# State-space parameters and rotation table on the Pool engine, eight state-space units started later, and small column work moved between engines, in a hybrid recurrent decoder step

## The chip, the cores and the metric

One core of a Trainium2 chip runs the whole program in one launch. The metric is device microseconds from start to end of an execution, lower is better. PE is the matrix engine, DVE the vector engine, ACT the scalar (activation) engine, POOL the general engine that the code calls `G` (`nc.gpsimd`), SP the engine that issues the DMAs. In the code `PE`, `V`, `S` and `G` stand for PE, DVE, ACT and POOL.

## What is computed

One step of a decoder layer on 544 tokens (one prompt of 512, and 8 samples of 4), 1,024 channels, float32, cut to what matters here:

```python
z = x @ w_in                                   # then split into 9 parts
# A: gated linear recurrence on 512 channels
xa_c = causal_conv4(xa);  gx, ga = sigmoid(gate matmuls of xa_c)
a  = exp(-8 * ga * softplus(-lambda))
bx = sqrt(1 - a*a) * (gx * xa_c)
h[t] = a[t]*h[t-1] + bx[t];   out_a = (h * gelu(ya)) @ proj_a
# B: short gated convolution
out_b = (sb * causal_conv3(sc * sh)) @ proj_b
# C: diagonal complex state space, 32 groups of 16 channels, 64 states each
step = exp(log_dt);  abar = exp(step * (a_re + i*a_im))
bbar = (abar - 1) / (a_re + i*a_im) * b
s[t] = abar * s[t-1] + bbar @ u[t];   y = Re(c @ s) + d * u
out_c = glu(gelu(y)) @ proj_c
x = LN(alpha*x + sigmoid-gated merge of out_a, out_b, out_c @ w_out)
x = LN(alpha*x + mlp(x))
```

The last states of A, B and C are outputs too.

## The kernel before

Every float32 matmul is done in three passes over a high and a low half of each operand. For the weights, the high half is an ACT cast (`wh`, L114 and later L819) and the low half a DVE subtraction (`wl`, L115 and L820). Weights are split two blocks ahead.

The program first computes `us`, the input of C, and then 20 blocks of `z`, one after the other, numbered by `ti`: 0 to 7 alternate between `xa` (with the convolution, `a_conv`) and `ya` (`gy`, a gelu on ACT), 8 to 11 are `sb`, 12 to 19 alternate between `sc` and `sh`. 20 to 27 are merge blocks. The text calls them tiles. One tile is 48 matmuls (two halves of the tokens, eight blocks of channels, three passes) into one of four rotating PSUM buffers (`big`), and ACT or DVE takes the result out. After tile `ti`, `run_side(ti)` writes out the side work that the table `at(...)` has put there; this table, and the order of the code, set the order on each engine, for each engine runs its instructions in the order in which they stand. The side work is:

- the gates of branch A (`a_gate`, after tiles 2, 4, 6, 8): a pair of small matmuls, on ACT three tanh (`tx` L607, `ta` L611, `aT` L612), on DVE `bx` (L608); then `a_rec` (DVE: r = 1 - t, reciprocal, product), `a_sqrt` (ACT, `q`), `a_coef` (POOL 2r - 1 into `aT`, DVE product), `a_scan` (tile 13: DVE scans along the tokens, and ACT copies of the last columns into the state tile `st`, L639 and L642);
- the parameters of C (`params`, called ahead of the tiles, on DVE) and the rotation table `E_r`, `E_i` (`etable`, 128 powers per state by doubling: six operations for each of 7 steps m, steps 0 to 3 on DVE, 4 to 6 on POOL);
- eight units of C, each of two groups of states: `ssm_w` and `ssm_o` (POOL: coefficient matrices `wt` and `oo`), `ssm_a` (PE: four transposes and eight small matmuls; ACT copies `W`, and ten blocks into `M`; DVE adds the diagonal D to `M`, L479, twice), `ssm_b` (PE matmuls with `W`; DVE products with the table, scans, products; POOL adds `HP`), `ssm_c` (ACT copies of the last state column out of `HP`, L517 and L518; PE with `M`, `oo` and `HP`; ACT gelu). The lists `UA`, `UB`, `UC` name the tile after which a, b and c of each unit stand.

Large tiles (`gy`, `sbt`, `q`, `r`, `E_r`, `Et`, ...) come from a pool `slot` of 14 buffers, in turn: a new tile takes the buffer of the oldest one and waits for its last reader. All small values of `params` lie in one such tile, named `scr`; so do the sines and cosines that `etable` reads (`cn`, `sn`), up to its last step.

After the tiles come Strassen-like sums of the inputs `xq` (`t_sum`, four DVE subtractions of 128x1088) and of the weights `sr` (POOL), and the merges. The lines that matter most:

```python
UA = [10, 13, 15, 18, 20, 22, 23, 25]
UB = [a + 1 for a in UA]
UC = [a + (2 if a > 18 else 3) for a in UA]
...
            e = V if m < 4 else G
...
        S.copy(W.rearrange("p r j n -> p (r j n)"), wps)
...
        S.copy(st_lh[:, :, 0:NB], prev)
...
        S.copy(two(sbt[:, ct]), flat(ps))
```

Of the kernel before, what the change touches and what calls it, by code (L numbers as in the profile page):

```python
# [64 lines left out]
def kernel(ctx: ExitStack, tc: tile.TileContext, I, O):  # L65
# [185 lines left out]
    def precise_exp(dst, v, n, name):  # L251
# [3 lines left out]
        ts(V, r, v, -87.0, 88.0, ALU.max, ALU.min)
        ts(V, k, r, 1.4426950408889634, MAGIC, MUL, ADD)
        ts(V, k, k, MAGIC, None, SUB)
        V.scalar_tensor_tensor(r, k, -0.693359375, r, op0=MUL, op1=ADD)
        V.scalar_tensor_tensor(r, k, 2.12194440e-4, r, op0=MUL, op1=ADD)
# [1 line left out]
        ts(V, dst, r, cs[7], cs[6], MUL, ADD)
        for c in cs[5::-1]:
            tt(V, dst, dst, r, MUL)
            ts(V, dst, dst, c, None, ADD)
        ts(V, ii, k, 127.0, 8388608.0, ADD, MUL)
        tt(V, dst, dst, ii.bitcast(F32), MUL)
# [3 lines left out]
    def params():  # L270
# [52 lines left out]
        tt(V, r2, angf, angf, MUL)  # L323
        f = [1.0 / math.factorial(i) for i in range(13)]
        ts(V, snf, r2, f[9], -f[7], MUL, ADD)
        for c in (f[5], -f[3], 1.0):
            tt(V, snf, snf, r2, MUL)
            ts(V, snf, snf, c, None, ADD)
        tt(V, snf, snf, angf, MUL)
        ts(V, cnf, r2, -f[10], f[8], MUL, ADD)  # L330
        for c in (-f[6], f[4], -f[2], 1.0):
            tt(V, cnf, cnf, r2, MUL)
            ts(V, cnf, cnf, c, None, ADD)
        t4 = stemp(128)
        ts(V, t4, kk, 0.25, MAGIC, MUL, ADD)
        ts(V, t4, t4, MAGIC, None, SUB)
        V.scalar_tensor_tensor(kk, t4, -4.0, kk, op0=MUL, op1=ADD)
        V.scalar_tensor_tensor(t4, kk, -1.0, kk, op0=MUL, op1=ALU.max)
# [1 line left out]
        ts(V, ck, t4, -1.0, 1.0, MUL, ADD)  # L340
        ts(V, t4, t4, -1.0, 2.0, MUL, ADD)
        tt(V, kk, kk, t4, MUL)
        ta, tb = stemp(128), stemp(128)
        tt(V, ta, snf, kk, MUL)
        tt(V, tb, cnf, kk, MUL)
        tt(V, cnf, cnf, ck, MUL)
        tt(V, cnf, cnf, ta, SUB)
        tt(V, snf, snf, ck, MUL)
        tt(V, snf, snf, tb, ADD)
# [7 lines left out]
        def cmul(orr, oi, ar, ai, br, bi):  # L357
            tt(V, u1, ar, br, MUL)
            tt(V, u2, ai, bi, MUL)
            tt(V, orr, u1, u2, SUB)  # L360
            tt(V, u1, ar, bi, MUL)
            tt(V, u2, ai, br, MUL)
            tt(V, oi, u1, u2, ADD)

        tt(V, A_r[:, :, 0], mag, cn[:, 0], MUL)
        tt(V, A_i[:, :, 0], mag, sn[:, 0], MUL)
# [4 lines left out]
        tt(V, rho, mag, mag, MUL)  # L371
        tt(V, rho, rho, rho, MUL)
        dn, nr = stemp(16), stemp(16)
        tt(V, u1, C("are"), C("are"), MUL)
        tt(V, u2, C("aim"), C("aim"), MUL)
        tt(V, dn, u1, u2, ADD)
        V.reciprocal(dn, dn)
        ts(V, nr, A_r[:, :, 0], 1.0, None, SUB)
# [1 line left out]
        tt(V, u1, nr, C("are"), MUL)  # L380
        tt(V, u2, ni, C("aim"), MUL)
        tt(V, u1, u1, u2, ADD)
        tt(V, F_r[:, :, 3], u1, dn, MUL)
        tt(V, u1, ni, C("are"), MUL)
        tt(V, u2, nr, C("aim"), MUL)
        tt(V, u1, u1, u2, SUB)
        tt(V, F_i[:, :, 3], u1, dn, MUL)
# [1069 lines left out]
```

## Time and profile before

| | |
|---|---|
| median of 3 runs | 882.92 us (882.62 to 883.97) |
| the profiled execution | 881.24 us, its span 879.5 us |
| PE busy | 841.5 us, 96% of the span |
| DVE busy | 637.6 us (73%) |
| ACT busy | 370.4 us (42%) |
| POOL busy | 306.1 us (35%) |
| mean granted TensorE clock | 0.987 |
| chain that ended last, by engine | PE 65%, DVE 22%, issue 4%, ACT 4%, DMA 3%, POOL 2% |

Times of the profile are in the span's own microseconds. The rest of the profiled execution, 1.7 us, lies around the span. A granted clock of 1.00 is 2.4 GHz, 0.50 is 1.2 GHz; a mean between them is a stretch that had both.

### The profile page before, as it was taken

To read this page: it belongs to the slowest core of one execution; us is meant where nothing else is said; L and a number is where in the kernel's file an instruction comes from. 1 tells how busy PE (TensorE), PEld (TensorE's weight loads), DVE (VectorE), ACT (ScalarE), POOL (GpSimd) and SP (SyncE) were. 2 spreads that over 40 slices of the span, in tenths; PEclk is the share of its full clock that TensorE was granted. 3 is DMA by queue.
4 is the path that set the end of the run, shared out by engine and by line. 5 is a ranking of instruction groups with operands and counts; after the bars stand their busy time and mean duration, and the time that the engine had idled before them with its cause. 6 is when DMAs were issued, how large, how long until landed. Compare 5 with 4: busy or idle time off the path is not lost.

```text
span 879.5 us, 16024 instructions
## 1 busy us (share of the span) xinstructions
PE 841.5 (96%) x6516; PEld 831.1 (94%) x6516; DVE 637.6 (73%) x1036; ACT 370.4 (42%) x626; POOL 306.1 (35%) x289
## 2 busy tenths in 40 slices
PE   7998869989999899989999999999999999999996
PEld 7997769989999899989998999999999999999996
DVE  6879998876565866689857889666666666655656
ACT  4352515343333543454435775444344444444310
POOL 1044963764652354844000321322221313132122
PEclk9999989999999999999999999999999999999998
DMA  8341123122214353223645435333333333333302
GB/s 296 124 118 48 52 75 104 54 75 82 77 50 137 129 139 98 72 72 96 221 160 175 144 124 168 96 97 97 96 97 96 98 96 96 91 90 126 104 4 100
DMA packets 31594, 94.00 MB, mean 107 GB/s; under 512 B 3424, under 2 KB 9952, under 8 KB 31136
## 3 DMA queue, kind: packets, MB, share of 16 engines
q1 hardware_dynamic: 31232, 91.92, 33.1%
q8 instruction: 51, 0.84, 0.4%
q0 software_dynamic: 288, 1.05, 0.3%
q14 instruction: 23, 0.19, 0.1%
HBM read 88.24 MB, written 2.49 MB: 103 GB/s over the span
## 4 chain that ended last, share of the span: by engine, by line
PE 65%; DVE 22%; issue 4%; ACT 4%; DMA 3%; POOL 2%; SPq 0%; DVEq 0%; ACTq 0%; POOLq 0%
PE big L146 37%; PE big L854 22%; DVE wl L115 4%; ACT wh L114 1%; DVE scr L233 1%; PE big L1284 1%; PE big L1125 1%; DMA raw<-in_w_dram 1%; DVE bx L233 1%; DVE wl L820 1%; DVE cacc L591 1%; DVE r L625 1%; DMA xraw<-in_xT_dram 1%; POOL sr L233 1%; DVE rl L233 1%
## 5 line engine op out<-in xcount | busy, mean ns | idle before, releaser
L233 POOL TENSOR_TENSOR sr<-raw 128x512 f32<-128x512 f32 x38 | 61.1, 1630 | 243.2 <-DMA raw<-in_w_dram 172.4
L146 PE MATMUL big<-xh,wh 128*128 128x272 f32 (+2 forms) x544 | 117.0, 297 | 6.6 <-DVE wh L196 4.6
L854 PE MATMUL big<-Tt,wh 128*128 128x272 f32 x608 | 118.0, 291 | 3.8 <-DVE uu L233 1.9
L115 DVE TENSOR_TENSOR wl<-raw,wh 128x1024 fp32r<-128x1024 f32 x70 | 90.7, 1299 | 37.3 <-ACT wh L114 37.3
L146 PE MATMUL big<-xh,wl 128*128 128x272 f32 (+2 forms) x544 | 113.9, 291 | 2.9 <-DVE wl L820 2.9
L146 PE MATMUL big<-xl,wh 128*128 128x272 f32 (+2 forms) x544 | 114.1, 292 | 0.0
L820 DVE TENSOR_TENSOR wl<-raw,wh 128x1024 fp32r<-128x1024 f32 (+1 forms) x73 | 96.2, 1318 | 20.1 <-ACT wh L819 19.0
L819 ACT CAST wh<-raw 128x1024 fp32r<-128x1024 f32 (+1 forms) x73 | 68.4, 937 | 84.6 <-PE big L146 47.3
L854 PEld LDWEIGHTS big<-Tt,wh 128*128 128x128 f32 x608 | 96.8, 191 | 4.6 <-DVE uu L233 2.1
L146 PE MATMUL big<-fh,wh 128*128 128x272 f32 (+2 forms) x448 | 98.2, 289 | 0.6 <-ACT rl L1178 0.6
L146 PE MATMUL big<-fh,wl 128*128 128x272 f32 (+2 forms) x448 | 97.8, 288 | 0.0
L146 PE MATMUL big<-fl,wh 128*128 128x272 f32 (+2 forms) x448 | 97.7, 288 | 0.0
L114 ACT CAST wh<-raw 128x1024 fp32r<-128x1024 f32 x70 | 73.0, 1046 | 57.9 <-PE big L146 37.2
L146 PEld LDWEIGHTS big<-xh,wh 128*128 128x128 f32 x544 | 87.1, 193 | 7.6 <-ACT xh L195 4.5
L146 PEld LDWEIGHTS big<-xh,wl 128*128 128x128 f32 x544 | 86.0, 192 | 3.2 <-DVE wl L820 3.2
L854 PE MATMUL big<-Tt,wl 128*128 128x272 f32 x304 | 88.8, 292 | 0.0
L146 PEld LDWEIGHTS big<-xl,wh 128*128 128x128 f32 x544 | 86.5, 192 | 0.1
L146 PEld LDWEIGHTS big<-fh,wh 128*128 128x128 f32 x448 | 72.4, 188 | 0.9 <-ACT rl L1178 0.8
L820 DVE TENSOR_TENSOR wl<-sr,wh 128x1024 fp32r<-128x1024 f32 x38 | 48.1, 1267 | 34.5 <-ACT wh L819 34.5
L146 PEld LDWEIGHTS big<-fl,wh 128*128 128x128 f32 x448 | 72.4, 188 | 0.0
L146 PEld LDWEIGHTS big<-fh,wl 128*128 128x128 f32 x448 | 72.1, 189 | 0.0
L819 ACT CAST wh<-sr 128x1024 fp32r<-128x1024 f32 x38 | 39.6, 1044 | 72.0 <-POOL sr L233 60.1
(299 smaller groups left out, 2075.4 us busy)
## 6 DMA issues: line engine op xcount, KB each, us to landing
raw<-in_w_dram SPq DMA_DIRECT2D x147, 512.0 KB, 3.6
xq<-in_xT_dram SPq DMA_DIRECT2D x2, 1088.0 KB, 6.4
xraw<-in_xT_dram SPq DMA_DIRECT2D x3, 544.0 KB, 7.7
raw<-in_w_dram SPq DMA_DIRECT2D x3, 384.0 KB, 6.9
x<-in_xT_dram SPq DMA_DIRECT2D x2, 576.0 KB, 5.4
U<-us_t SPq DMA_DIRECT2D x16, 68.0 KB, 3.7
zc<-Y SPq DMA_DIRECT2D x16, 68.0 KB, 3.8
bc<-in_bc_dram SPq DMA_DIRECT2D x8, 128.0 KB, 3.2
```

The costliest lines, as they stand in the source:

```text
L114: S.copy(h, r)
L115: V.tensor_tensor(l, r, h.bitcast(F32), op=SUB)
L146: PE.matmul(out, w, x[:, a:b], start=first and oi == 0, stop=last and oi == 2)
L233: e.tensor_tensor(o, a, b, op=op)
L591: V.scalar_tensor_tensor(acc, xp[:, k:568 + k], w(k), acc, op0=MUL, op1=ADD)
L625: V.reciprocal(r, r)
L819: S.copy(h[:, 0:n], src)
L820: V.tensor_tensor(l[:, 0:n], src, h[:, 0:n].bitcast(F32), op=SUB)
L854: PE.matmul(out, w[:, sl], y[:, k], start=k == 0 and oi == 0, stop=k == 3 and oi == 2)
L1125: PE.matmul(out, x, w[:, sl], start=first and kk == 0 and oi == 0, stop=kk == K - 1 and oi == 2)
L1284: PE.matmul(out[:, 256 * e:256 * e + 256], x, w[:, sl], start=False, stop=e == 1 and k == 3 and oi == 2)
```

## The change

Seven things change:

1. The parameters of C beyond `step` and one reciprocal are a function of their own, `params_ssm`, put after tile 0, with all its operations on POOL. [...]
2. All seven steps of `etable` are on POOL, and it stands after tile 1 where it stood after tile 2.
3. The units stand later: a of the first after tile 13 instead of 10, and c always two tiles behind a.
4. D: instead of two DVE operations on `M`, POOL makes a small block `dq` (32x64), and DVE adds it to the product in PSUM before ACT copies `M` from there.
5. `nci` is made in place in the loaded block `bc`.
6. The state columns: out of `HP` by one POOL copy in `ssm_b` (two ACT copies in `ssm_c` before), and `st_lh` by DVE (ACT before). The two copies into `HP` become one.
7. 1 - t and 2r - 1 of branch A are ACT operations (DVE and POOL before), and `t_sum` runs on POOL.

```diff
-UA = [10, 13, 15, 18, 20, 22, 23, 25]
+UA = [13, 15, 17, 19, 21, 22, 24, 25]
 UB = [a + 1 for a in UA]
-UC = [a + (2 if a > 18 else 3) for a in UA]
+UC = [a + 2 for a in UA]
...
+    def fma(e, o, a, c, b, t, op=ADD):
+        ts(e, t, a, c, None, MUL)
+        tt(e, o, t, b, op)
...
+    def params_ssm():
+        step, dn = P["step"], P["dn"]
         mag = stemp(16)
         va = stemp(16)
-        tt(V, va, step, C("are"), MUL)
-        precise_exp(mag, va, 16, "e1")
+        tt(G, va, step, C("are"), MUL)
+        precise_exp(G, mag, va, 16, "e1")
...
-            e = V if m < 4 else G
+            e = G
...
-        nci = s2.tile([128, 2, 32], F32, tag="nci", name="nci")
-        ts(G, nci, q["bc"][:, :, 3], -1.0, None, MUL)
+        nci = q["bc"][:, :, 3]
+        ts(G, nci, nci, -1.0, None, MUL)
+        dq = s2.tile([128, 2, 32], F32, tag="dq", name="dq")
+        sh = [32, 2, 32]
+        tt(G, dq[96:128], ident[96:128, 96:128].unsqueeze(1).to_broadcast(sh),
+           C("d", 2 * u, 2 * u + 2)[96:128].unsqueeze(2).to_broadcast(sh), MUL)
...
-        for s in range(4):
-            for sp in range(s, 4):
-                qd = 3 - (sp - s)
+        tt(V, kps[96:128, 0:64], kps[96:128, 0:64], q["dq"][96:128].rearrange("p j c -> p (j c)"), ADD)
+        for qd in range(4):
+            for s in range(qd + 1):
+                sp = s + 3 - qd
                 S.copy(M[32 * s:32 * s + 32, :, 32 * sp:32 * sp + 32],
                        kps[32 * qd:32 * qd + 32, 0:64].rearrange("p (j c) -> p j c", j=2))
-        for j in range(2):
-            V.scalar_tensor_tensor(M[:, j], ident, C("d", 2 * u + j, 2 * u + j + 1), M[:, j], op0=MUL, op1=ADD)
...
+        G.tensor_copy(st_s[:, :, j0:j0 + 2, 8], HP[:, :, :, 136])
...
-        S.copy(st_sr[:, 2 * u:2 * u + 2, 8:9], HP[:, 0, :, 136:137])
-        S.copy(st_si[:, 2 * u:2 * u + 2, 8:9], HP[:, 1, :, 136:137])
...
+                if "r" not in AQ:
+                    AQ["r"] = stile(name="r")
+                S.activation(AQ["r"][:, ct], aT[:, ct], AF.Identity, bias=one[:, 0:1], scale=-1.0)
...
-        ts(V, r, aT[:, ct], -1.0, 1.0, MUL, ADD)
         V.reciprocal(r, r)
...
-        ts(G, aT[:, ct], AQ["r"][:, ct], 2.0, -1.0, MUL, ADD)
+        S.activation(aT[:, ct], AQ["r"][:, ct], AF.Identity, bias=one[:, 1:2], scale=2.0)
...
-        S.copy(st_lh[:, :, 0:NB], prev)
+        V.tensor_copy(st_lh[:, :, 0:NB], prev)
...
-    at(2, etable)
+    at(0, params_ssm)
+    at(1, etable)
...
-        tt(V, d, e, f, SUB)
+        tt(G, d, e, f, SUB)
```

Two places show what this does to the order on the engines. In brackets stand the engines and queues whose semaphores an instruction waits for.

The first is ACT around the first copy out of an `sb` tile (tile 8, `sbt`) and the last gate. Before:

```order
L114 CAST wh<-raw 128x1024 [waits DMAHW3_49,PE_49]
L701 COPY sbt<-big 128x544 [waits DMAHW6_49,DMAHW5_49,DMAHW7_49,DMAHW4_49,PE_49]
L607 ACTIVATE tx<-big,hb 128x544 [waits DVE_49,PE_49]
L611 ACTIVATE ta<-big,hb 128x544 [waits PE_49]
L612 ACTIVATE aT<-ta,c_435 128x544 [waits Activation_49]
L618 ACT_TABLE_LOAD [waits Activation_49]
L618 ACTIVATE q<-aT 128x2176 [waits Pool_49]
L114 CAST wh<-raw 128x1024 [waits DMAHW4_49,PE_49]
L701 COPY sbt<-big 128x544 [waits PE_49]
L639 COPY st<-bx 128x4x8 [waits DVE_49]
L114 CAST wh<-raw 128x1024 [waits DMAHW5_49,PE_49]
```

And now:

```order
L114 CAST wh<-raw 128x1024 [waits DMAHW3_49,PE_49]
L718 COPY sbt<-big 128x544 [waits PE_49,Pool_49]
L625 ACTIVATE tx<-big,hb 128x544 [waits DVE_49,PE_49]
L629 ACTIVATE ta<-big,hb 128x544 [waits PE_49]
L630 ACTIVATE aT<-ta,c_444 128x544 [waits Activation_49]
L633 ACTIVATE r<-aT,one 128x544 [waits Activation_49]
L637 ACT_TABLE_LOAD
L637 ACTIVATE q<-aT 128x2176 [waits Pool_49]
L645 ACTIVATE aT<-r,one 128x544 [waits Activation_49]
L718 COPY sbt<-big 128x544 [waits PE_49]
L645 ACTIVATE aT<-r,one 128x544
L114 CAST wh<-raw 128x1024 [waits DMAHW4_49]
```

The first `sbt` copy waited for DMAs that free a buffer, and now waits for POOL: the pool of 14 now gives `sbt` the buffer of `scr`, whose last reader is the last but one operation of `etable`. The copy of `st` from `bx`, which stood ahead of a cast of weights, is gone from ACT.

The second is POOL where C's parameters come in. Before:

```order
L506 COPY HP<-cp 128x2x8
L237 TENSOR_SCALAR nci<-bc 128x64 [waits DMAHW7_49]
L237 TENSOR_SCALAR nci<-bc 128x64 [waits DMAHW0_49]
L233 TENSOR_TENSOR oo<-A_r,bc 128x256 [waits DVE_49]
L233 TENSOR_TENSOR oo<-A_r,nci 128x256 [waits Pool_49]
```

And now, at the start of the parameters:

```order
L242 TENSOR_SCALAR bc<-bc 128x2x32 [waits DMAHW7_49]
L242 TENSOR_SCALAR bc<-bc 128x2x32 [waits DMAHW0_49]
L238 TENSOR_TENSOR scr<-scr,cp 128x16 [waits DVE_49]
L238 TENSOR_TENSOR scr<-scr,cp 128x16
L244 TENSOR_SCALAR scr<-scr 128x16 [waits Pool_49]
L242 TENSOR_SCALAR scr<-scr 128x16 [waits Pool_49]
L242 TENSOR_SCALAR scr<-scr 128x16 x6
```

Where POOL waited for DVE to bring the parameters, it now makes them, after one wait for DVE (`step`). From that first `scr` operation to the last one that reads `scr` it has 179 instructions: 2 MEMSET and 65 TENSOR_TENSOR and 21 TENSOR_SCALAR of 16 columns, 6 of 32 and 6 of 64, 27 TENSOR_TENSOR and 20 TENSOR_SCALAR of 128, and TENSOR_TENSOR of 256 (21), 512 (6) and 1,024 columns (5).

The addition of `dq` stands on DVE among the steps of the convolution of branch B, and ACT's copies of `M` wait for it, where DVE's two operations on `M` waited for these copies before. The first `t_sum` stands on POOL ahead of the four sums of weights (`sr`), the other three behind them.

## Rows read from the trace of the kernel before

**Rows 1.** Stretches: busy us (count) of PE, PEld, DVE, ACT, POOL; PEclk; DMA; GB/s.

```profile
30.00:108.00 78.00, 70.67 (x521) 68.09 (x520) 70.03 (x205) 31.75 (x55) 38.82 (x35) 0.98 0.26 73
108.00:145.00 37.00, 29.14 (x222) 28.93 (x222) 33.94 (x44) 10.82 (x29) 16.29 (x17) 0.91 0.23 76
```

**Rows 2.** What PE waited for, 25 to 200 us: total, times, longest.

```profile
PE big L489 <- ACT W L471: 9.9, 2, 7.9
PE big L605 <- ACT tx L607: 6.4, 2, 3.7
PE big L146 <- ACT sc L716: 1.1, 1, 1.1
PE big L523 <- POOL HP L233: 0.2, 1, 0.2
```

**Rows 3.** What PE waited for, 280 to 320 us.

```profile
PE big L146 <- DVE wl L820: 2.9, 1, 2.9
```

**Rows 4.** What ACT waited for, whole run.

```profile
ACT st L517 <- POOL HP L233: 51.4, 8, 9.5
```

**Rows 5.** ACT in time: start, us, instruction, count, idle before it and releaser.

```profile
127.98 0.25 ACT L639 COPY st<-bx 128x32 f32<-128x32 f32 x1 [17.50 <-DVE bx L233]
...
129.59 0.59 ACT L471 COPY W<-big 128x512 f32<-128x512 f32 x1
```

**Rows 6.** PE in time, from the last gate to the end of tile 13.

```profile
99.22 3.62 PE L605 MATMUL big<-xc,gw 128*128 128x272 f32 x8 [3.69 <-ACT tx L607]
114.36 0.41 PE L146 MATMUL big<-xl,wh 128*128 128x272 f32 x2
114.61 0.42 PE L146 MATMUL big<-xh,wl 128*128 128x272 f32 x2
...
130.23 2.18 PE L489 MATMUL big<-U,W 128*128 128x136 f32 x8 [7.86 <-ACT W L471]
...
144.83 0.39 PE L521 MATMUL big<-U,M 128*128 128x136 f32 x2
```

**Rows 7.** Ten-us stretches of the same kind as rows 1.

```profile
130.00:140.00 10.00, 9.77 (x65) 9.78 (x66) 9.97 (x17) 4.12 (x16) 0.00 (x0) 0.81 0.34 107
...
190.00:200.00 10.00, 7.97 (x52) 7.75 (x51) 7.40 (x14) 6.37 (x20) 7.77 (x9) 0.83 0.21 66
```

**Rows 8.** DVE in time: the last step of `step`, and two operations alone and beside POOL.

```profile
29.98 0.18 DVE L233 TENSOR_TENSOR scr<-scr,e0i 128x20 f32<-128x20 f32 x1
...
86.04 1.16 DVE L115 TENSOR_TENSOR wl<-raw,wh 128x1024 fp32r<-128x1024 f32 x1
...
88.84 2.07 DVE L115 TENSOR_TENSOR wl<-raw,wh 128x1024 fp32r<-128x1024 f32 x1
```

**Rows 9.** POOL in time: steps of the table, and a small product.

```profile
79.75 0.61 POOL L233 TENSOR_TENSOR Et<-E_i,scr 128x256 f32<-128x256 f32 x1
...
83.90 1.05 POOL L233 TENSOR_TENSOR Et<-E_r,scr 128x512 f32<-128x512 f32 x1
...
95.89 1.89 POOL L233 TENSOR_TENSOR Et<-E_i,scr 128x1024 f32<-128x1024 f32 x1
...
102.85 2.10 POOL L233 TENSOR_TENSOR Et<-E_i,scr 128x1024 f32<-128x1024 f32 x1
```

**Rows 10.** POOL by form, 0 to 300 us: busy us, mean ns, idle before.

```profile
L506 POOL COPY HP<-cp 128x16 f32<-128x16 f32 x8 | 1.6, 195 | 0.0
L233 POOL TENSOR_TENSOR fb<-A_i,cp 128x128 f32<-128x128 f32 x2 | 0.9, 433 | 13.9 <-PE big L489 13.9
```

**Rows 11.** POOL in time, while DVE was busy beside it.

```profile
115.83 0.99 POOL L239 TENSOR_SCALAR aT<-r 128x544 f32<-128x544 f32 x1 [3.17 <-DVE r L625]
116.79 2.13 POOL L233 TENSOR_TENSOR wt<-F_r,bc 128x256 f32<-128x256 f32 x2
...
125.88 0.37 POOL L237 TENSOR_SCALAR nci<-bc 128x64 f32<-128x64 f32 x1
```

**Rows 12.** The tile `HP`: its adds on POOL, ns min, median, max.

```profile
L233 POOL TENSOR_TENSOR HP<-xx,xy x10: 729/736/1663, 141.4 to 226.7; 128x256 f32<-128x256 f32 x10
```

More of the change, by code (lines that the diff above doesn't have):

```diff
@@ L159 @@
     V.memset(warm, 0.0)
+    one = const.tile([128, 2], F32, name="one")
+    V.memset(one[:, 0:1], 1.0)
+    V.memset(one[:, 1:2], -1.0)
     S.activation(warm, warm, AF.Tanh)
@@ L249, in stemp, with precise_exp @@
         return scr["t"][:, o:o + n]
[L251 removed]
+    def fma(e, o, a, c, b, t, op=ADD):
+        ts(e, t, a, c, None, MUL)
+        tt(e, o, t, b, op)
+    def precise_exp(e, dst, v, n, name):
         k = stemp(n)
         r = stemp(n)
+        t = stemp(n)
         ii = ptile(n, name + "i", I32)
[L255 to L259, printed above, removed]
+        ts(e, r, v, -87.0, 88.0, ALU.max, ALU.min)
+        ts(e, k, r, 1.4426950408889634, MAGIC, MUL, ADD)
+        ts(e, k, k, MAGIC, None, SUB)
+        fma(e, r, k, -0.693359375, r, t)
+        fma(e, r, k, 2.12194440e-4, r, t)
         cs = [1.0 / math.factorial(i) for i in range(8)]
[L261 removed]
+        ts(e, dst, r, cs[7], cs[6], MUL, ADD)
         for c in cs[5::-1]:
[L263 to L266, printed above, removed]
+            tt(e, dst, dst, r, MUL)
+            ts(e, dst, dst, c, None, ADD)
+        ts(e, ii, k, 127.0, 8388608.0, ADD, MUL)
+        tt(e, dst, dst, ii.bitcast(F32), MUL)
     P = {}
@@ L275, in params @@
         V.scalar_tensor_tensor(ev[:, 16:20], C("lam"), -1.0, C("lam"), op0=MUL, op1=ALU.min)
-        precise_exp(ex, ev, 20, "e0")
+        precise_exp(V, ex, ev, 20, "e0")
         step, e = ex[:, 0:16], ex[:, 16:20]
+        dn, d2 = stemp(16), stemp(16)
+        tt(V, dn, C("are"), C("are"), MUL)
+        tt(V, d2, C("aim"), C("aim"), MUL)
+        tt(V, dn, dn, d2, ADD)
+        V.reciprocal(dn, dn)
+        P.update(step=step, dn=dn)
         den = stemp(4)
@@ L322, in params @@
         sn, cn = (x.rearrange("p (f j) -> p f j", f=8) for x in (snf, cnf))
-        tt(V, r2, angf, angf, MUL)
+        tt(G, r2, angf, angf, MUL)
         f = [1.0 / math.factorial(i) for i in range(13)]
-        ts(V, snf, r2, f[9], -f[7], MUL, ADD)
+        ts(G, snf, r2, f[9], -f[7], MUL, ADD)
         for c in (f[5], -f[3], 1.0):
[L327 to L330, printed above, removed]
+            tt(G, snf, snf, r2, MUL)
+            ts(G, snf, snf, c, None, ADD)
+        tt(G, snf, snf, angf, MUL)
+        ts(G, cnf, r2, -f[10], f[8], MUL, ADD)
         for c in (-f[6], f[4], -f[2], 1.0):
[L332 to L338, printed above, removed]
-        ck = stemp(128)
[L340 to L349, printed above, removed]
+            tt(G, cnf, cnf, r2, MUL)
+            ts(G, cnf, cnf, c, None, ADD)
+        ts(G, t4, kk, 0.25, MAGIC, MUL, ADD)
+        ts(G, t4, t4, MAGIC, None, SUB)
+        ta, tb = stemp(128), stemp(128)
+        fma(G, kk, t4, -4.0, kk, ta)
+        ts(G, ta, kk, 0.0, 2.0, ALU.max, MUL)
+        tt(G, t4, ta, kk, SUB)
+        ck = stemp(128)
+        ts(G, ck, t4, -1.0, 1.0, MUL, ADD)
+        ts(G, t4, t4, -1.0, 2.0, MUL, ADD)
+        tt(G, kk, kk, t4, MUL)
+        tt(G, ta, snf, kk, MUL)
+        tt(G, tb, cnf, kk, MUL)
+        tt(G, cnf, cnf, ck, MUL)
+        tt(G, cnf, cnf, ta, SUB)
+        tt(G, snf, snf, ck, MUL)
+        tt(G, snf, snf, tb, ADD)
         A_r = const.tile([128, 16, 4], F32, name="A_r")
@@ L357, in cmul @@
         def cmul(orr, oi, ar, ai, br, bi):
[L358 to L366, printed above, removed]
+            tt(G, u1, ar, br, MUL)
+            tt(G, u2, ai, bi, MUL)
+            tt(G, orr, u1, u2, SUB)
+            tt(G, u1, ar, bi, MUL)
+            tt(G, u2, ai, br, MUL)
+            tt(G, oi, u1, u2, ADD)
+        tt(G, A_r[:, :, 0], mag, cn[:, 0], MUL)
+        tt(G, A_i[:, :, 0], mag, sn[:, 0], MUL)
         cmul(A_r[:, :, 1], A_i[:, :, 1], A_r[:, :, 0], A_i[:, :, 0], A_r[:, :, 0], A_i[:, :, 0])
@@ L370, in params @@
         rho = ptile(16, "rho")
[L371 to L378, printed above, removed]
-        ni = A_i[:, :, 0]
[L380 to L387, printed above, removed]
+        tt(G, rho, mag, mag, MUL)
+        tt(G, rho, rho, rho, MUL)
+        nr = stemp(16)
+        ts(G, nr, A_r[:, :, 0], 1.0, None, SUB)
+        ni = A_i[:, :, 0]
+        tt(G, u1, nr, C("are"), MUL)
+        tt(G, u2, ni, C("aim"), MUL)
+        tt(G, u1, u1, u2, ADD)
+        tt(G, F_r[:, :, 3], u1, dn, MUL)
+        tt(G, u1, ni, C("are"), MUL)
+        tt(G, u2, nr, C("aim"), MUL)
+        tt(G, u1, u1, u2, SUB)
+        tt(G, F_i[:, :, 3], u1, dn, MUL)
         for s in range(3):
```

24 lines of the change are left out of this document (12 added, 12 removed).

## The prediction

> **What bounds the kernel now.** I read the busy table first: PE is busy for 96% of the span, so what can be won is what PE loses between its matmuls, and how the other engines' work is shared out matters only where PE waits for it. Next the waits of PE: between 25 and 200 us it waits 9.9 us in two stands for the ACT copy `W`, 6.4 us in two for the tanh `tx`, 1.1 us for `sc` and 0.2 us for `HP` [rows 2], and at 295 us 2.9 us for a `wl` on DVE [rows 3]. Next the stretches: from 30 to 108 us DVE is busy for 70.0 of 78 us, from 108 to 145 us for 33.9 of 37 us, while POOL has 39 of 78 and 16 of 37 us [rows 1]. So these waits are DVE's: `tx` waits for buffers and inputs that DVE brings late. The longest is less direct. ACT stands for 17.50 us before the small copy of `st` from `bx`, because the DVE scans of branch A come late; the cast of weights and the copy `W` are queued behind it on ACT, `W` runs at 129.59, and PE begins only at 130.23 after 7.86 us of nothing [rows 5, 6].
>
> A stand costs more than its own length. After the 7.86 us the eight matmuls of b take 2.18 us, and the mean granted clock of 130 to 140 us is 0.81; of 190 to 200 us, with the second stand for `W`, 0.83 [rows 6, 7]. Between the levels of 1.2 and 2.4 GHz, 0.81 over 10 us means 3.8 us at the lower one, so half of that, 1.9 us, is lost; 0.83 means 1.7 us. The last gate, after its stand of 3.69 us, takes 3.62 us, which would be 1.8 at the upper level [rows 6].
>
> All of it together: 9.9 + 6.4 + 1.1 + 0.2 + 2.9 us of waits and 1.9 + 1.7 + 1.8 us of clock, 25.9 us. That is the most that the change can win.
>
> **The change, part by part.** *DVE and ACT are relieved.* The parameters, steps 0 to 3 of the table, two operations on `M` per unit, r = 1 - t and the sums leave DVE, and the `st` copies leave ACT. With them go the `tx` waits, the stand of 17.50 us on ACT, and with the copies of the state column the 51.4 us in eight waits that ACT spends on `HP` ahead of other work [rows 4, 5]. ACT gets eight operations of 544 columns, of which it has room for far more. The new addition of `dq` is 64 columns on DVE per unit, under 0.2 us by the 20-column operation of 0.18 [rows 8]; it stands ahead of the `M` copies, whose matmuls come two tiles later. The in-place `nci`, the merged `HP` copies and the `dq` product of POOL are a few tenths on an engine that waits there. I cost all of these at nothing; their cover is the two tiles of 6 us between a and c.
>
> *POOL gets a chain that PE must now wait for.* This decides. The order shows that the first `sbt` copy (tile 8) now waits for POOL, because it is given the buffer of `scr`, and `scr` is read up to the last but one operation of the table. Behind that copy stand on ACT the last gate's `tx`, `ta`, `aT`, then `r`, `q` and the further casts; and PE's tile 10 needs the PSUM buffer that this copy empties, for tile 8, the two halves of the gate and tile 9 hold all four. So PE stops in front of tile 10 until POOL has read `scr` for the last time. Call that moment T. Before, the table's last read of `scr` ended at 104.95 [rows 9], and nothing needed it that soon.
>
> T is worked out as follows. POOL can begin when DVE has made `step`, at 29.98 + 0.18, say 30.3 [rows 8]. Its 179 operations, by rows without much beside them: products of 256 columns take 0.61, of 512 1.05, of 1,024 about 1.95 [rows 9], of 128 columns 0.43 [rows 10]. The line through 128 and 256 columns is 0.25 + 1.4 ns a column, so 0.27 for 16 columns, 0.30 for 32, 0.34 for 64. A one-tensor operation takes 0.37 at 64 columns and 0.99 at 544 [rows 11], so 0.31 at 16 and 0.45 at 128. The sum: 65 x 0.27 + 21 x 0.31 + 6 x 0.30 + 6 x 0.34 + 27 x 0.43 + 20 x 0.45 + 21 x 0.61 + 6 x 1.05 + 5 x 1.95, with two MEMSETs of 0.1, is 77 us. No row shows a 16-column product on POOL; the nearest is a copy of 16 columns at 0.195 [rows 10], and by it the 86 small ones would be 7 us cheaper: 70. Gaps where a step waits for the one before (112 of them wait for POOL's own result) could add 5: 82. I take 77, since these are products, like the rows of 128 columns, and not copies.
>
> Then DVE disturbs it. From 115.83 to 125.88 POOL ran one operation of 544 columns and eight products of 256, about 6.2 us by the prices above, in 10.05 us; two products together took 2.13 instead of 1.22 [rows 11]. DVE's two-tensor operations in that stretch come to some 5 to 6 us, so POOL lost about 0.7 us for each us of them; in the other direction a `wl` took 2.07 instead of 1.16 beside POOL [rows 8]. Up to the stop DVE has ten `wl` (1.16) and eighteen operations of about 550 columns (half of that), 22 us. POOL loses 0.7 of it, 15.5 us; the bounds are 10 (half of them meet a POOL operation) and 22 (all of it). So T = 30.3 + 77 + 15.5 = 123, between 110 and 134.
>
> The "SBUF — State Buffer" page of the Trainium skill (Who interferes with whom) says that a DVE instruction with two SBUF inputs contends with a POOL instruction that reads SBUF, that the lock is exclusive, and that the loser blocks fully. Rows 11 agree in kind and show less than the whole; by the rule in full, T would be the 130 of the second rival below.
>
> PE without stands would come to tile 10 at about 100: its end, 114.61 + 0.25, less 6.05 for the tile (24 pairs that begin 0.25 apart), less the 6.4 of `tx` and the 1.8 of clock [rows 2, 6]. So it stands for some 23 us instead of 7.86.
>
> *From T on.* The copy takes 0.6 us, PE begins at T + 0.75. Tile 10 costs 6.05 and again 1.9 for the clock, then tiles 11 to 13: it is through tile 13 at T + 26.85. Before, this was at 144.83 [rows 6], and a and b of the first unit had been done by then, about 2.1 us (b is half of 2.18, a about as much), which still lie ahead now. The shift there is T + 26.85 + 2.1 - 144.83 = T - 115.9. What lies behind it and goes away: the second `W` wait (9.9 - 7.9 = 2.0), its 1.7 of clock, `sc` 1.1, `HP` 0.2 and the 2.9 of `wl`, together 7.9, since ACT no longer waits for `HP` and DVE no longer makes the sums ahead of that `wl`. What comes anew: c stands one tile, 6 us, behind b, while b's DVE chain (four products of 512 columns, two of 256, four short scans, some 4.5 to 5 us) and two adds of 0.74 on POOL [rows 12] come to 6.5 to 7. PE waits about 1 us for each of the first three units, and 0.7 at the sums, 3.7 in all (bounds 0 and 8).
>
> The change is therefore T - 115.9 - 7.9 + 3.7 = T - 120.1. With T = 123 it is +3 us. Against the profiled execution, 881.24, that is 884; this one lies 1.7 below the median of 882.92, so in terms of the median **886 us**.
>
> **The rivals.** *POOL is lighter than costed.* The small operations cost what the copy does (70 us) and DVE takes 10 us from POOL: T = 110, the change is -10, the time 873. For it speaks that the rows of 128 and 256 columns may overstate the base cost, against it the 112 waits in the chain. The point from which this decides is T = 120. Between 117 and 123 the result is close to nothing.
>
> *Full contention.* POOL gives way for all of the 22 us: T = 130, +10, 892; with gaps besides, T = 134, +14, 897. For it speaks that POOL's operations are now short, so that DVE rarely has to wait long before it gets through; against it, rows 11.
>
> *The table isn't late.* If T came before 100, or if the buffer of `scr` were free for another reason, all of the 25.9 would be won less 3.7: -22, 861. The rows would have to be wrong by a quarter; and DVE's operations could then not meet POOL at all.
>
> *DVE is the bound in tiles 14 to 20.* Units now follow each other every two tiles, and the b chains push `wl` and convolutions: the 3.7 becomes 8, +7 in all, 890.
>
> **How the numbers follow.** As costed (T from 114 to 128, 880 to 891) 0.52; lighter 0.20; full contention 0.18; the table not late 0.05; DVE the bound 0.05. A measurement of this kernel can tell about 0.2%, 1.8 us, from no change. Of the 0.52 some 0.10 lies below T = 118.3 (faster), 0.12 between 118.3 and 121.9 (the same), and 0.30 above. Faster is 0.10 + 0.20 + 0.05 = 0.35, the same 0.12, slower 0.30 + 0.18 + 0.05 = 0.53. The range from 873 to 898 takes in the bounds of T from 110 to 134 and leaves out the table that isn't late and the outer halves of two rivals. Both signs hold much of the chance; the likeliest case alone has 880 to 891.
>
> **What would show it.** Right: one long stand of PE in front of tile 10, about 20 us, released by ACT's `sbt`, ACT idle ahead of it, released by POOL; POOL busy without a break from 30 to about 123 us, the clock low in the tile behind the stand; no stand for `W` and none for `tx`. Sixteen-column products of POOL at about 0.27. Wrong: a PE that goes through tile 10 at about 100 us without a stop, or a POOL that is done well before 113 us, or waits of over 4 us for `HP`, `W` or `wl` in tiles 14 to 27.

## The result, and the profile after

The changed kernel takes 903.18 us (median of 4, 902.57 to 906.05), the kernel before beside it 883.44 us (882.62 to 884.06): 1.0237 times as long, interval 1.0220 to 1.0254. Forecast were 886 us and a range up to 898. The direction was right, with a chance of 0.53 hardly better than a coin's; the place of the largest wait was right too; the size was short by 17 us. "After" is the changed kernel from here on, "before" the kernel before.

The waits of PE after, from 25 to 200 us and from 280 to 345 us (engine, line, tile, releaser: us in total, times, longest), answer to [rows 2, 3]:

```profile
PE big L146 <- ACT sbt L718: 28.7, 1, 28.7
PE big L538 <- POOL HP L238: 3.0, 2, 2.0
PE big L539 <- POOL HP L238: 2.5, 2, 1.2
...
PE big L146 <- DVE rl L238: 2.7, 1, 2.7
PE big L871 <- ACT t L966: 2.2, 2, 1.8
PE big L146 <- DVE wl L837: 1.4, 1, 1.4
```

A third unit adds 0.8 us for `HP` at 208 us, so `HP` has 6.3 in all. Both `W` waits, both `tx` waits and the one for `sc` are gone, as costed. In their place stands one of 28.7 us. Its chain in time (start, us, instruction, and the idle time before it with its releaser), on POOL, ACT and PE:

```profile
30.36 0.40 POOL L238 TENSOR_TENSOR scr<-scr,cp 128x16 f32<-128x16 f32 x2 [7.95 <-DVE scr L238]
...
97.40 0.24 POOL L238 TENSOR_TENSOR Et<-E_r,scr 128x16 f32<-128x16 f32 x1
...
124.79 1.90 POOL L238 TENSOR_TENSOR Et<-E_i,scr 128x1024 f32<-128x1024 f32 x1
126.77 2.36 POOL L238 TENSOR_TENSOR E_i<-Et 128x1024 f32<-128x1024 f32 x1
```

```profile
126.72 0.61 ACT L718 COPY sbt<-big 128x544 f32<-128x544 f32 x1 [35.05 <-POOL Et L238]
```

```profile
127.39 0.82 PE L146 MATMUL big<-xh,wh 128*128 128x272 f32 x2 [28.70 <-ACT sbt L718]
```

POOL works from 30.36 on its chain with no gap but those between one operation and the next; the last operation that reads `scr` ends at 126.69; 0.03 us later ACT's copy begins, and PE's tile 10 after that. In the stretches that answer to [rows 1] (same columns) DVE and ACT stand idle with PE, and the granted clock of 0.67 says that PE both stood and came back at the lower level:

```profile
30.00:108.00 78.00, 68.68 (x523) 67.21 (x521) 43.08 (x63) 29.36 (x52) 71.00 (x166) 0.96 0.28 83
108.00:145.00 37.00, 17.61 (x122) 17.61 (x123) 16.24 (x22) 12.95 (x16) 20.43 (x15) 0.67 0.04 15
```

**One account for all kernels.** I cut each profile into stretches of 5 us and summed two things from 30 to 860 us: the time in which PE is not busy, and its busy time times (1 - granted clock). Two of the stretches after (columns: PE busy with count, PEclk, DMA, GB/s):

```profile
130.00:135.00 5.00, 5.00 (x33) 0.74 0.00 0
190.00:195.00 5.00, 4.50 (x24) 0.66 0.35 105
```

The first counts 1.3 us as lost to the clock, the second 0.5 us idle and 1.5 us lost. What remains of the span is nearly the same in all kernels here, 845.5 to 847.4 us: the work of PE itself, and the ends before 30 and behind 860 us. So a time is explained when its idle and its clock column are. The last four columns are of one execution, the profiled one, and the clock column moves between executions: ten of e5 had mean granted clocks of 0.981 to 0.992 and took 885.34 to 877.43 us, so a few us in that column alone don't show an effect of an edit. Ratios are to the kernel before in the same runs.

| kernel | median us | ratio (95%) | span | PE idle | lost to clock | rest |
|---|---|---|---|---|---|---|
| before | 883.44 | 1 | 879.5 | 25.9 | 6.6 | 847.0 |
| after | 903.18 | 1.0237 (1.0220 to 1.0254) | 901.5 | 47.2 | 7.5 | 846.8 |
| e1 own buffers | 892.70 | 1.0125 (1.0099 to 1.0150) | 892.3 | 36.0 | 9.3 | 847.0 |
| e2 sines and cosines only | 902.79 | 1.0235 (1.0209 to 1.0262) | 900.9 | 41.4 | 13.3 | 846.2 |
| e3 sums on DVE | 901.08 | 1.0218 (1.0194 to 1.0242) | 900.6 | 44.1 | 10.0 | 846.5 |
| e4 c three later | 895.37 | 1.0159 (1.0138 to 1.0180) | 893.5 | 43.4 | 4.6 | 845.5 |
| e5 parameters on DVE | 883.87 | 1.0005 (0.9983 to 1.0028) | 882.1 | 22.5 | 12.7 | 846.9 |
| e6 table split | 912.03 | 1.0356 (1.0317 to 1.0394) | 908.4 | 51.6 | 9.4 | 847.4 |
| e7 before, `st` off ACT | 879.14 | 0.9969 (0.9956 to 0.9981) | 877.4 | 24.6 | 7.3 | 845.5 |
| e8 without POOL's parts | 872.76 | 0.9890 (0.9857 to 0.9924) | 871.6 | 18.9 | 5.4 | 847.3 |
| e9 as e8, table on POOL | 871.60 | 0.9876 (0.9854 to 0.9899) | 869.5 | 17.0 | 5.5 | 847.0 |
| e10 as e8, sums on POOL | 878.08 | 0.9951 (0.9931 to 0.9972) | 875.9 | 21.1 | 9.0 | 845.8 |
| e11 as e8, old places | 877.36 | 0.9941 (0.9924 to 0.9958) | 874.0 | 18.0 | 10.2 | 845.8 |
| e12 POOL's parts with room | 874.83 | 0.9927 (0.9911 to 0.9944) | 870.2 | 18.4 | 5.3 | 846.5 |

After against before: 21.3 us more idle, 0.9 us more lost to the clock.

### The profile page after: what moved, and what is told of

The parts are those of the page before. It is cut to its first block, busy times and chain, and to the rows that moved or that the text cites. A ratio compares the mean times of both kernels' runs of the same rounds, so it can differ in the third digit from the quotient of the medians.

```text
span 901.5 us, 16029 instructions
## 1 busy us (share of the span) xinstructions
PE 842.1 (93%) x6516; PEld 832.1 (92%) x6516; DVE 592.0 (66%) x888; ACT 374.7 (42%) x616; POOL 365.9 (41%) x442
## 3 DMA queue, kind: packets, MB, share of 16 engines
q0 software_dynamic: 288, 1.05, 0.3%
## 4 chain that ended last, share of the span: by engine, by line
PE 67%; POOL 14%; DVE 10%; issue 3%; ACT 3%; DMA 2%; SPq 0%; DVEq 0%; ACTq 0%; POOLq 0%
PE big L146 40%; PE big L871 21%; POOL scr L238 3%; DVE wl L115 2%; POOL Et L238 2%; POOL sr L238 2%; POOL scr L242 1%; DMA raw<-in_w_dram 1%; PE big L1301 1%; PE big L1142 1%; POOL xq L238 1%; POOL HP L238 1%; ACT wh L114 1%; POOL scr L244 1%; DMA xraw<-in_xT_dram 1%
## 5 line engine op out<-in xcount | busy, mean ns | idle before, releaser
L146 PE MATMUL big<-xh,wh 128*128 128x272 f32 (+2 forms) x544 | 116.5, 296 | 33.3 <-ACT sbt L718 28.7
L115 DVE TENSOR_TENSOR wl<-raw,wh 128x1024 fp32r<-128x1024 f32 x70 | 89.8, 1287 | 48.6 <-ACT wh L114 48.5
L837 DVE TENSOR_TENSOR wl<-raw,wh 128x1024 fp32r<-128x1024 f32 (+1 forms) x73 | 93.0, 1274 | 18.0 <-ACT wh L836 17.1
```

Source lines behind the costliest of these rows:

```text
L115: V.tensor_tensor(l, r, h.bitcast(F32), op=SUB)
L146: PE.matmul(out, w, x[:, a:b], start=first and oi == 0, stop=last and oi == 2)
L837: V.tensor_tensor(l[:, 0:n], src, h[:, 0:n].bitcast(F32), op=SUB)
```

## The experiments

### Is it the buffer of scr? (e1, e2)

e1 gives the sines, the cosines and the table's temporary buffers of their own. They are small tiles (`xx`, `X`, `xy`) that the first b uses later:

```diff
-        snf, cnf = stemp(128), stemp(128)
+        scx = s1.tile([128, 2, 2, 128], F32, tag="xx", name="xx")
+        snf, cnf = scx[:, 0, 0], scx[:, 0, 1]
...
-        et = stile(shape=(128, 2, 16, 64), name="Et")
-        t1, t2 = et[:, 0], et[:, 1]
+        t1 = s1.tile([128, 2, 2, 128], F32, tag="X", name="X").rearrange("p r j n -> p (r j n)").rearrange("p (j n) -> p j n", j=16)
+        t2 = s1.tile([128, 2, 2, 128], F32, tag="xy", name="xy").rearrange("p r j n -> p (r j n)").rearrange("p (j n) -> p j n", j=16)
         for m in range(7):
             n = 1 << m
+            for o in range(0, n, 32):
...
```

> The changed kernel, with the sines and cosines and the table's temporary in small tiles that branch C's first b uses later, so that neither the first sbt copy nor q waits for the table; the step of 64 columns is done in two halves for that. Everything else is as changed. Theory 1 (the stand of 28.7 us in front of tile 10 is nothing but the buffer of scr): PE goes through tiles 10 to 13 without a stand and begins a of the first unit at 98.7 + 4 x 6.05 = 123 us where it did at 153.8; the table is done at about 130, when b of the first unit is; time 903 - 31 = 872. Rival (POOL's lateness is the cause, whatever the buffer): the wait comes back at b of the first unit or at wt and oo of the next units, over 10 us of PE standing between 120 and 180 us, time 885 or more.

Measured: 892.70, ratio 1.0125: 10 us gained on the change (0.0112 x 881) of the 31, the rival's outcome. PE goes through tiles 10 to 13 without a stand, as theory 1 has it, and then stands at c of the first unit. On PE, DVE and POOL of this run:

```profile
157.81 0.59 PE L541 MATMUL big<-HP,oo 128*128 128x136 f32 x1 [20.44 <-POOL HP L238]
```

```profile
146.20 0.69 DVE L238 TENSOR_TENSOR xx<-big,E_r 128x512 f32<-128x512 f32 x1 [10.25 <-POOL xy L238]
```

```profile
98.01 0.23 POOL L238 TENSOR_TENSOR X<-E_r,xx 128x16 f32<-128x16 f32 x1
...
123.99 2.10 POOL L238 TENSOR_TENSOR xy<-E_i,xx 128x512 f32<-128x512 f32 x1
...
145.12 1.05 POOL L238 TENSOR_TENSOR xy<-E_i,xx 128x512 f32<-128x512 f32 x1
146.25 1.26 POOL L238 TENSOR_TENSOR E_i<-X,xy 128x512 f32<-128x512 f32 x1
```

The table begins at the same time as after (98.0 against 97.4) but ends at 147.5 instead of 129.1: 49.5 us instead of 31.7. The halved last step explains 1.3 us of it (two times 6.9 against 12.5). The other 16 are DVE's: after, DVE stood idle all that time, for it waited for ACT; here it runs up to 136 us. The same product takes 2.10 us at 124 beside DVE and 1.05 at 145, when DVE stands. So the stand of 28.7 us had kept DVE out of POOL's way, and taking it away brought most of it back a few tiles later. The first b waits here for the borrowed tile, free at 146.2, and then for `E_i`, done at 147.5, so the borrowing itself changes little.

e2 moves the sines and cosines alone (the first hunk):

> The changed kernel, with only the sines and cosines moved out of scr: the sbt copy waits for the last parameter (about 88 us) and no longer for the table, but q, next on ACT, still waits for the table's last operation (129 us). Theory 1: the stand moves behind q, PE gets through tiles 10 and 11 and stands ahead of tile 12 for the cast that is queued behind q, until about 137 us; it gains 4 of the 31 us, time 899. Rival (only the copy counts): 872 as in the run before.

Measured: 902.79 against 1.0237 times its kernel before, 901.6: nothing gained, where 4 us were expected. The stand is behind `q`, where theory 1 puts it: 17.9 us, then more behind it.

```profile
134.00 0.82 PE L146 MATMUL big<-xh,wh 128*128 128x288 f32 x2 [17.89 <-ACT wh L114]
```

```profile
129.06 2.02 ACT L638 ACTIVATE q<-aT 128x2176 f32<-128x2176 f32 x1 [33.28 <-POOL E_i L238]
```

The idle time did fall, by 5.8 us, and the time lost to the clock rose by as much (7.5 to 13.3). One long stand had become several; that this is why is argued, not shown.

### The length of POOL's chain (e5, e6)

From here theory 2: what costs is that POOL's chain ends too late, whichever instruction shows the wait.

e5 puts all operations of `params_ssm` on DVE (`V` in the place of `G`), where each multiply-add is one operation and not two:

```diff
+        if e is V:
+            V.scalar_tensor_tensor(o, a, c, b, op0=MUL, op1=op)
+            return
         ts(e, t, a, c, None, MUL)
```

> The changed kernel with only the parameters of C back on DVE (with its fused operations); the whole table stays on POOL, everything else as changed. Theory 2 (the length of POOL's chain is what costs, wherever its wait shows): 121 operations leave POOL, the table runs from about 66 us and scr is read for the last time at about 103; the stand in front of tile 10 falls from 28.7 to under 5 us, some 3 us of waits for tx come back: 20 us under the changed kernel (881 to 884). Rival (DVE then is late by as much as POOL was): over 12 us of waits for tx, W and sbt together before 150 us, less than 12 us gained.

Measured: 883.87, ratio 1.0005, 20 us under the changed kernel. The stand is gone altogether, for POOL has done the table at 89 us; waits for `gy` and `tx` of 1.6 and 3.6 us are back. POOL and PE:

```profile
86.72 2.38 POOL L238 TENSOR_TENSOR E_i<-Et 128x1024 f32<-128x1024 f32 x1
```

```profile
82.85 1.73 PE L626 MATMUL big<-xc,gw 128*128 128x272 f32 x3 [3.61 <-ACT tx L628]
```

e6, only steps 0 to 3 of the table back on DVE:

```diff
-            e = G
+            e = V if m < 4 else G
```

> The changed kernel with steps 0 to 3 of the table back on DVE, the parameters still on POOL. These steps took POOL 8 us (97.4 to 105.5). Theory 2: T goes from 126.7 to about 119, the stand from 28.7 to about 21 us, 8 us gained on the changed kernel. Rival (POOL's chain isn't what PE waits for in the end): nothing gained.

Measured: 912.03, ratio 1.0356, 10 us slower than the changed kernel (0.0119 x 882) where 8 less were expected. Neither theory nor rival had it. DVE and ACT:

```profile
84.65 0.19 DVE L238 TENSOR_TENSOR Et<-E_r,scr 128x16 f32<-128x16 f32 x1 [39.05 <-POOL E_i L412]
```

```profile
94.53 0.71 ACT L625 ACTIVATE tx<-big,hb 128x544 f32<-128x544 f32 x1 [42.65 <-DVE xc L611]
```

The first step on DVE reads what POOL's memsets of `E_r` and `E_i` write, and those stand on POOL behind the whole chain of parameters. DVE takes its instructions in order, so it stood for 39 us with the convolution `xc` behind it; behind `xc` waited `tx` on ACT, and PE stood for 32 us ahead of the second gate. The four steps themselves took DVE 5 us (84.65 to 89.8), and POOL's chain did end earlier, at 120. I had counted what leaves POOL and not what DVE must then wait for.

### The other parts (e3, e4, e7, e8, e10, e11)

e3:

```diff
-        tt(G, d, e, f, SUB)
+        tt(V, d, e, f, SUB)
```

> The changed kernel with the four sums of the inputs back on DVE. Theory 1: the waits of PE between 305 and 405 us for wl, t, rl and rl (1.4 + 2.2 + 2.7 + 1.4 = 7.7 us) come from POOL, which needs 2.2 to 2.9 us for each sum and makes three of them behind the sums of weights; all but the wait for wl go (that grows from 1.4 to 2.9): 903 - 5 = 898. Rival (these waits come from the units standing later, not from the sums): no change, 902 to 904.

Measured: 901.08, ratio 1.0218, its interval overlapping that of the change: not separated. The waits for `t` and for the first `rl` are gone and the one for `wl` is 2.6, as expected; the second `rl` (1.5) stays, so it doesn't come from the sums on POOL, and 2.5 us more are lost to the clock in this execution. What the sums cost stays open here; e10 repeats the question on a kernel without the long stand.

e10 is e8 (below) with the sums on POOL:

> The run without POOL's costly parts, but with the four sums on POOL. Theory: the waits for t and rl come back at 300 to 325 us, about 2.2 + 2.7 us, and the wait for wl falls from 2.7 to 1.4: 3 to 5 us more than that run, 876 where before is 882. Rival (the sums cost nothing on POOL, the waits come from elsewhere): equal, 872 to 874.

Measured: 878.08 (0.9951) against 0.9890: 5 us more, and the waits are at the places named:

```profile
299.22 0.39 PE L874 MATMUL big<-xh,wh 128*128 128x272 f32 x1 [1.85 <-ACT t L969]
...
314.18 0.52 PE L146 MATMUL big<-ah,wh 128*128 128x272 f32 x2 [2.59 <-DVE rl L238]
```

Three sums take 8.75 us on POOL, behind the sums of weights, and with them come late the cast `Tt` on ACT and the copies `t` behind it. After, on POOL:

```profile
311.01 8.75 POOL L238 TENSOR_TENSOR xq<-xq 128x1088 f32<-128x1088 f32 x3
```

e4:

```diff
-UC = [a + 2 for a in UA]
+UC = [a + (2 if a > 18 else 3) for a in UA]
```

> The changed kernel with c of the first three units three tiles behind a again. Theory 1: the waits for HP (3.6 + 2.7 us) go, 903 - 6 = 897, and the clock of 190 to 200 us stays up (another 1 us). Rival (DVE is what is short in tiles 14 to 20, c's place only shows it): the waits move to wl or W, 902 to 904.

Measured: 895.37, ratio 1.0159, 7 us under the change (0.0078 x 881), as theory 1 has it. The 6.3 us for `HP` are gone. Half of them come back, though, as the rival has it, in other places than it names: 3 us for `bh` and `bl`, the high and low half of branch B's result, at 210. In this execution 2.9 us less are lost to the clock.

e7 is the kernel before with `V.tensor_copy` for both `st_lh` copies, and

```diff
+        G.tensor_copy(st_s[:, :, j0:j0 + 2, 8], HP[:, :, :, 136])
...
-        S.copy(st_sr[:, 2 * u:2 * u + 2, 8:9], HP[:, 0, :, 136:137])
-        S.copy(st_si[:, 2 * u:2 * u + 2, 8:9], HP[:, 1, :, 136:137])
```

> The kernel before with one part of the change alone: the state columns off ACT (st_lh copied by DVE, the last column of HP by one POOL copy). Theory: ACT no longer stands 17.5 us before 128 us, so the stand of 7.86 us for W and its 1.9 us of clock go, and the 2.0, 1.1 and 0.2 us of later waits with 1.7 of clock go too: 14 us at most; what DVE itself is late by (the scans of branch A end at 128) comes back at c of the first unit, so 8 to 12 us under the kernel before. Rival (DVE is late and W only shows it): the waits move to wl or HP, under 3 us gained.

Measured: 879.14, ratio 0.9969: 3 us, at the rival's bound. The stand of 7.86 us for `W` [rows 6] is now one of 8.55 us for `HP`; what is won is about the second `W` wait (2.0) and the one for `sc` (1.1).

```profile
142.59 0.82 PE L522 MATMUL big<-HP,oo 128*128 128x136 f32 x2 [8.55 <-POOL HP L234]
```

So the copy of `st`, which the chain of [rows 5, 6] shows at the front of ACT's queue, was not what the first unit lacked: DVE, late with branch A and busy without a break from 108 to 141 us, was.

e8, the changed kernel with e3, e4 and e5 together, and

```diff
-            e = G
+            e = V if m < 4 else G
...
-    at(1, etable)
+    at(2, etable)
```

> The changed kernel without its three costly parts: the parameters and steps 0 to 3 of the table on DVE, the sums on DVE, c of the first three units three tiles behind a, table after tile 2 as before; kept are the later units, D in PSUM, nci in place, the state columns and 1 - t off ACT and DVE. Theory: no stand in front of tile 10, none for W, about 3 us for tx and 3 for wl; 12 to 16 us under the kernel before. Rival (the kept parts win nothing, since DVE is the bound until 145 us): within 3 us of the kernel before.

Measured: 872.76, ratio 0.9890, 10 us under before, less than the 12 to 16 expected. From 103 to 188 us PE doesn't wait; 7.9 us for `tx` and `gy` are left ahead of that.

e11 is e8 with `UA` and `UC` of before:

> The run without POOL's costly parts, but with the units where they were before (a of the first after tile 10). Theory: DVE's backlog of branch A (its scans end at about 128) meets the first unit again, PE waits 5 to 9 us for HP or W before 145 us; 6 to 10 us more than that run, 880 where before is 882. Rival (the later places win nothing, D in PSUM and the copies do it): within 2 us of that run.

Measured: 877.36 (0.9941), 4.5 us more than e8, the two intervals just meeting at 0.9924. The stand is where it was expected, of 4.3 us:

```profile
141.10 0.82 PE L541 MATMUL big<-HP,oo 128*128 128x136 f32 x2 [4.31 <-POOL HP L238]
```

By the medians the later places are worth nearly half of what e8 wins. The account doesn't show where: PE is idle 0.9 us less in e11 than in e8, and of the 4.8 us more that it loses to the clock 3.2 lie between 75 and 105 us, where PE and DVE have the same work in both kernels. What D, `nci` and 1 - t on ACT win by themselves was not run; with the copies of the state columns they make the 5 us that e11 lies under before, and those copies alone made 3 in e7.

### What beats both (e9, e12)

e9 is e5 with e3 and e4: the parameters on DVE, the whole table on POOL.

> The run without POOL's costly parts, but with the whole table on POOL (parameters and sums on DVE, c three tiles behind a, table after tile 1). DVE loses 24 operations before tile 10. In the run with the parameters alone on DVE, PE waited 5.2 us for tx and gy against 7.9 without POOL's parts, and POOL was done with the table at 89 us. Theory: with c later and the sums on DVE its 6.2 us for HP and its clock go; 1 to 3 us less than the run without POOL's parts, 870 where before is 882. Rival (the contention of POOL's longer chain with DVE costs as much as DVE is relieved): equal to that run, 872 to 874, or slower.

Measured: 871.60 (870.93 to 871.95), ratio 0.9876: the fastest here, 1.2% under before; e8's interval overlaps it. On POOL the table begins at 45.5 us here and is done at 89:

```profile
45.52 0.27 POOL L238 TENSOR_TENSOR Et<-E_r,scr 128x16 f32<-128x16 f32 x1 [22.70 <-DVE xp L598]
...
86.76 2.37 POOL L238 TENSOR_TENSOR E_i<-Et 128x1024 f32<-128x1024 f32 x1
```

Begun that early, the table on POOL costs nothing that can be told from e8.

e12 leaves parameters and table on POOL, with e1's buffers and e3, and

```diff
-UA = [13, 15, 17, 19, 21, 22, 24, 25]
-UC = [a + 2 for a in UA]
+UA = [16, 17, 19, 20, 21, 22, 24, 25]
+UC = [a + (2 if a > 18 else 3) for a in UA]
```

> Parameters and whole table on POOL as in the changed kernel, but with room for them: own buffers for the sines, cosines and the table's temporary (as in the run with own buffers), a of the units after tiles 16, 17, 19, 20, 21, 22, 24, 25, c of the first two three tiles behind a, the sums on DVE. In the run with own buffers the table was done at 147.5 us, when PE would be at the end of tile 16 or 17. Theory 2: nothing asks for the table before it is there; the 20 us for HP go, the waits for tx don't come back since DVE has no parameters, 868 to 872 where before is 882. Rival (the crowded units, with DVE and POOL both full until 200 us, cost it again): 10 us or more of waits for HP, W or wl between 145 and 230 us, 876 or more.

Measured: 874.83, ratio 0.9927, 7 us under before and 27 under the change. This lies between the 872 of theory 2 and the 876 of the rival. Theory 2 holds for the stand: with nothing asking for the table before it is there, PE no longer stands in front of tile 10. But POOL's parts are not free: by the ratios e9 is 4 to 5 us faster, its interval clear of this one. POOL and PE:

```profile
148.12 2.13 POOL L238 TENSOR_TENSOR E_i<-X,xy 128x512 f32<-128x512 f32 x1
```

```profile
201.65 0.50 PE L541 MATMUL big<-HP,oo 128*128 128x136 f32 x2 [3.79 <-POOL HP L238]
```

PE doesn't wait before 148 us (no `tx`, `gy` or `sbt`), then 5.3 us for `W` and `wt` and 4.5 us for `HP`, 3.8 of it in one stand, in units that stand close: with 9.8 us of such waits much of the rival is in it.

## Why the prediction was right and wrong

**Right: where and why.** ACT's first `sbt` copy waits for POOL, PE stands in front of tile 10, and no stand for `W` or `tx` is left. T was to be 123 and is 126.7. PE came to tile 10 at 98.7, and through tile 13 at 153.8 (T + 26.85 gives 153.55). Up to that point the sum is right to 4 us, all of them T's.

T came so close partly by luck, for its terms were off in both directions. As written they add up to 77.6, not 77, which makes T 123.4. A 16-column product takes 0.20 to 0.25 us undisturbed, less than the 0.27 of the extrapolation; but a group of six in the table takes 1.65 (97.40 to 99.05), since a step that waits for the one before leaves a gap. The table, undisturbed, took 29.3 us to its last read of `scr`; by the prices it was to take 27.8, and 2.0 us of it are such gaps. What stands ahead of it, parameters and the first unit's matrices, took 67.0 against 65.3 with the contention. Here e6 helps, in which DVE stands from 45.6 us on. After and e6, from the first operation on `scr` to the first MEMSET of the table (columns as in [rows 1]):

```profile
30.36:97.20 66.84, 66.84 (x510) 65.58 (x509) 42.79 (x61) 29.36 (x52) 61.64 (x137) 1.00 0.33 97
30.57:84.49 53.92, 32.77 (x256) 32.24 (x254) 9.82 (x31) 9.91 (x19) 48.72 (x136) 0.85 0.19 51
```

POOL is idle between operations for 5.2 us in both, and busy for 12.9 us longer where DVE runs. PE stands in e6 too, from 63 us on, but that isn't it: the same seven products take 5.14 us after, and 3.10 in e6 with PE running and DVE and ACT idle. After, then e6:

```profile
63.09 5.14 POOL L238 TENSOR_TENSOR scr<-scr 128x128 f32<-128x128 f32 x7
```

```profile
59.84 3.10 POOL L238 TENSOR_TENSOR scr<-scr 128x128 f32<-128x128 f32 x7
```

So the gaps cost 7.3 us in all, where the sum took nothing (5 in its upper bound), and the contention at least 12.9 (DVE runs in e6 too, up to 45.6 us), where it took 15.5.

**Wrong: the two terms behind tile 13.** They were to give back 7.9 us and to cost 3.7. The 6.2 us of waits among the 7.9 did go.

- *What comes anew* was put at 3.7 us, with bounds 0 and 8, and is 14.0: 6.3 for `HP`, 1.4 + 2.2 + 2.7 for `wl`, `t` and `rl` around the sums, and 1.4 for a second `rl` at 400.7. For `HP` the step that failed is the time from b to c: I put 6.5 to 7 us, and for the first unit it takes 9.9, from the end of b's matmuls at 162.2 to the end of POOL's second add at 172.1. On PE, DVE, POOL and PE:

```profile
161.11 1.09 PE L507 MATMUL big<-U,W 128*128 128x136 f32 x8
```

```profile
161.76 1.10 DVE L238 TENSOR_TENSOR bl<-vv,bh 128x544 fp32r<-128x544 f32 x1 [0.77 <-ACT bh L725]
162.80 1.63 DVE L115 TENSOR_TENSOR wl<-raw,wh 128x1024 fp32r<-128x1024 f32 x1
...
164.46 0.69 DVE L238 TENSOR_TENSOR xx<-big,E_r 128x512 f32<-128x512 f32 x1
```

```profile
169.66 2.47 POOL L238 TENSOR_TENSOR HP<-xx,xy 128x256 f32<-128x256 f32 x2 [2.97 <-DVE xy L238]
```

```profile
170.44 0.50 PE L538 MATMUL big<-HP,oo 128*128 128x136 f32 x2 [2.03 <-POOL HP L238]
...
172.18 0.50 PE L539 MATMUL big<-HP,oo 128*128 128x136 f32 x2 [1.24 <-POOL HP L238]
```

  DVE's chain itself takes 5.1 us (164.46 to 169.58), close to the 4.5 to 5 of the sum. What the sum had at nothing is DVE's queue: `bl` and `wl` stand ahead, and the chain begins 2.3 us after b ends. And POOL's two adds take 2.5 us instead of 1.5. PE waits at each of them.

  For the sums I priced one wait of 0.7 us and nothing for the three that POOL makes behind the sums of weights; the three waits are 6.3 together. e4 (7 us) and e10 (5 us) show that both terms cost time. The second `rl` is there in e3, e5, e7, e8 and e9 too, whoever makes the sums, but not in e6 and e11, and before it was 0.2; what brings it stays open.
- *The clock* was to give back 1.7 us at the second `W` wait. Its wait went, but those for `HP` took its place: 190 to 200 us has 0.83 before [rows 7] and after. Two later stands, for `rl` at 339 us and for `uu` at 404, cost 1.7 us each, where before had one that cost 1.5.

The profiled executions are 22 us apart (903.31 and 881.24; the medians 19.7), and the sum had 3. So 3.7 (T) + 10.3 + 1.7 + 1.7 is 17.4 of the 19 us between 3 and 22; the rest I can't assign. The range failed with it: its upper end held T at 134 with the other terms at their middle, and not the sum of several terms on the expensive side. The sign of being wrong that I had named, over 4 us of waits for `HP`, `W` or `wl` in tiles 14 to 27, did come, with 6.3 us for `HP`; the rival behind it, DVE as the bound in tiles 14 to 20, had been given 0.05.

**Wrong too, though it didn't decide:** the rival in which the buffer is free for another reason was given the whole 25.9 us of before's losses. (That sum left out 0.9 us for `gy`, which stands in the same view as [rows 2], and 4.5 us of waits behind 345 us; that PE's idle column for before also reads 25.9 is chance.) e1 made the buffer free and won 10: the table is wanted again by the first b, and takes 16 us longer with DVE running. And "the table isn't late" was no matter of rows wrong by a quarter: e5 gets it by taking 121 operations off POOL, e12 by asking later. Most of what I took as ACT's fault before (the copy of `st`) was DVE's, as e7 shows.

The "SBUF — State Buffer" page of the Trainium skill (Who interferes with whom) would, taken in full, have had T at 130. The trace has 126.7, of which 7.3 us are gaps. The contention by itself was at least 12.9 us, against the 15.5 of my reading of [rows 11] and the 22 of the rule in full; how much it was up to 45.6 us, where DVE runs in e6 too, no run here shows.

## What to carry to other kernels

A chain moved to a slower engine must be timed to its last reader, and a buffer that is recycled counts as a reader: the first sign here was a copy that had nothing to do with the table. When such a wait is found, ask what is wanted next from the same chain before crediting the gain of removing it, and what the stand had kept out of the way. When a step moves between engines, look at what each queue then waits for at its front (e6), not only at the work that leaves; and when a chain is given a time, count what stands ahead of it in its queue.
